# Four strided loads in place of one at the head of a streaming contrast kernel

## The chip, the cores and the metric

The kernel runs on one core of a Trainium2 chip. The metric is the device time of one execution in microseconds. Before the change the median of three runs is 239.16 us (239.13 to 239.31).

## The reference

The input is a batch of 16 images of 3 channels, 512 x 512 pixels in float32, 50.33 MB in all. For each of the 48 channel planes the mean is taken, and every pixel is moved away from it by a factor and clipped:

```python
def reference(x, factor):
    mean = np.mean(x, axis=(2, 3), keepdims=True)
    return np.clip(mean + factor * (x - mean), 0, 1).astype(np.float32)
```

Since factor * x + (1 - factor) * mean is the same thing, each pixel needs one multiplication and one addition of a number that is constant in its plane, and then a maximum and a minimum. The factor is 1.5.

## The kernel before

The input is seen as one long array of rows of 8192 elements (32 KB). A plane is 32 rows, and a tile is 128 rows, one to each partition of SBUF: four planes and 4 MB. There are 12 tiles. SBUF holds a ring of six of them (`ring`, 128 x 6 x 8192), so that tile t lies in slot t mod 6, and it is computed in place: the loaded slot is overwritten with the result and stored from there.

For each tile `compute(t)` does the following. VectorE adds up columns 0 to 4351 of each row (line 81), and ScalarE, beside it, columns 4352 to 8191 (line 84, whose elementwise output `junk` isn't used). Two small matrix products on TensorE (lines 86 and 87) with the block matrix `blockw`, which holds (1 - factor) / pixels in blocks of 32 x 32, add the row sums of each plane and give every row of the plane its number (1 - factor) * mean, in PSUM. VectorE then computes factor * x + that number (line 91) and the clip (line 94), and ScalarE's queue issues the store (line 101).

The first tile is cut in two. Its columns 0 to 2047 (`SHORT`, 8 KB of each row, 1 MB) are loaded by a DMA of their own, the other 6144 columns (3 MB) by a second, both from `load` (line 76) on SyncE's queue. Lines 91, 94 and 101 run over the same two parts for the first tile, so that the 1 MB part can be stored before the rest is done. The sums of line 81 reach over both parts.

The order of the work is written out by hand. SyncE issues, one behind the other and with nothing to wait for, the 1 MB and the 3 MB of tile 0, tile 1 (4 MB), tiles 2 and 3 in one DMA (8 MB), and tiles 4 and 5 in one DMA (8 MB). Then follows the loop over the tiles, in which each `compute(t)` is followed by the load of tile t + 6 into the slot that tile t leaves. That load waits on SyncE until the store of tile t has finished. All loads are on SyncE's queue, all stores on ScalarE's.

Each DMA signals its end on one of eight completion semaphores, which the framework hands out in turn over the loads and stores of both queues; a DMA that gets a semaphore for the second time waits until its earlier holder has ended.

Of the kernel before, what the change touches and what calls it, by code (L numbers as in the profile page):

```python
# [1 line left out]

# [4 lines left out]


P = 128  # L10
ROW = 8192
BUFS = 6
SHORT = 2048
FIRST = (SHORT, ROW - SHORT)
SUM = 4352


@with_exitstack
def kernel(
    ctx: ExitStack,  # L20
    tc: tile.TileContext,
    x: bass.AP,
    factor: float,
    out: bass.AP,
):

    nc = tc.nc
    f32 = mybir.dt.float32  # L30
    Alu = mybir.AluOpType
    Act = mybir.ActivationFunctionType

    B, C, H, W = x.shape
    n_img, n_pix = B * C, H * W
    ppi = n_pix // ROW
    per_tile = P // ppi
    n_tiles = n_img // per_tile
    assert ppi * ROW == n_pix and per_tile * n_tiles == n_img

    factor = float(factor)
    wconst = (1.0 - factor) / float(n_pix)

    x_f = x.rearrange("b c h w -> (b c h w)")
    out_f = out.rearrange("b c h w -> (b c h w)")

    def dram(ap, t, c0=0, c1=ROW):
        return bass.AP(tensor=ap.tensor, offset=t * P * ROW + c0, ap=[[ROW, P], [1, c1 - c0]])

    consts = ctx.enter_context(tc.tile_pool(name="consts", bufs=1))  # L50
    xpool = ctx.enter_context(tc.tile_pool(name="xpool", bufs=1))
    small = ctx.enter_context(tc.tile_pool(name="small", bufs=1))
    psum = ctx.enter_context(tc.tile_pool(name="psum", bufs=1, space=bass.MemoryType.PSUM))


    sums = small.tile([P, 2 * n_tiles], f32, name="sums")
    junk = small.tile([P, ROW - SUM], f32, name="junk")
    bias = psum.tile([P, n_tiles], f32, name="bias")

    blockw = consts.tile([P, P], f32, name="blockw")  # L60
    nc.gpsimd.memset(blockw, 0.0)  # L61
    for a in range(0, P, ppi):
        nc.gpsimd.memset(blockw[a : a + ppi, a : a + ppi], wconst)  # L63


    ring = xpool.tile([P, BUFS, ROW], f32, name="ring")

    def load(t, c0=0, c1=ROW, n=1):

        b = t % BUFS  # L70
        src = bass.AP(
            tensor=x_f.tensor,
            offset=t * P * ROW + c0,
            ap=[[ROW, P], [P * ROW, n], [1, c1 - c0]],
        )
        nc.sync.dma_start(out=ring[:, b : b + n, c0:c1], in_=src)  # L76

    def compute(t):
        xt = ring[:, t % BUFS, :]
        own = sums[:, 2 * t : 2 * t + 2]  # L80
        nc.vector.tensor_reduce(  # L81
            out=own[:, 0:1], in_=xt[:, 0:SUM], axis=mybir.AxisListType.X, op=Alu.add
        )
        nc.scalar.activation(out=junk, in_=xt[:, SUM:ROW], func=Act.Copy, accum_out=own[:, 1:2])  # L84
        shift = bias[:, t : t + 1]
        nc.tensor.matmul(shift, blockw, own[:, 1:2], start=True, stop=False)  # L86
        nc.tensor.matmul(shift, blockw, own[:, 0:1], start=False, stop=True)  # L87
        c = 0
        for n in FIRST if t == 0 else [ROW]:
            part = xt[:, c : c + n]  # L90
            nc.vector.tensor_scalar(  # L91
                out=part, in0=part, scalar1=factor, scalar2=shift, op0=Alu.mult, op1=Alu.add
            )
            nc.vector.tensor_scalar(  # L94
                out=part, in0=part, scalar1=0.0, scalar2=1.0, op0=Alu.max, op1=Alu.min
            )
            store(t, c, c + n)
            c += n

    def store(t, c0, c1):  # L100
        nc.scalar.dma_start(out=dram(out_f, t, c0, c1), in_=ring[:, t % BUFS, c0:c1])

    with tc.manual_schedule():
        load(0, c1=SHORT)
        load(0, c0=SHORT)
        load(1)
        load(2, n=2)
        load(4, n=2)
        for t in range(n_tiles):
            compute(t)  # L110
            if t + BUFS < n_tiles:
                load(t + BUFS)


# [1 line left out]
_INS = ['x', 'factor']  # L116
_OUTS = [((16, 3, 512, 512), 'float32')]

_NUMBERS = {'factor': 1.5}


# [26 lines left out]
```

## Time and profile before

The profile is one execution. It spans 237.3 us between its first and its last instruction; the 239.16 us are the median of three other executions, measured from outside.

| | before |
|---|---|
| median of three runs | 239.16 us |
| span of the profiled execution | 237.3 us |
| VectorE busy | 163.1 us (69%) |
| ScalarE busy | 43.2 us (18%) |
| TensorE busy | 14.1 us (6%) |
| bytes read and written | 50.33 MB and 50.33 MB |
| mean rate over the span | 424 GB/s |
| packets on the load queue, on the store queue | 1840, 1872 |
| share of 16 engines' span, loads and stores | 49.7%, 49.2% |

The page draws the span as 40 slices, and the digit of a slice is the share in tenths in which a unit was busy. A packet is what one DMA engine moves at a time: here a whole row of up to 32 KB, or a small write to a completion semaphore. The two queues' shares add up to 98.9% of the time that all 16 engines have.

Windows of the profile give, for stretches of the span, the busy time of each compute engine and then the DMA share and GB/s. A packet is counted there with its start, so that short windows swing above and below the true rate. The list of issues gives, for each group of DMAs, its size and the time from issue to landing. The chain of waits follows the work that ended last back from the last instruction; its lines have a start, a duration and what it was.

### The profile page before, as it was taken

The page shows a single profiled execution, that of the slowest core. Times are in us where ns is not written, and L with a number is a line of the kernel's source. Part 1 is how long each engine was busy: PE and PEld are TensorE (multiplying, and loading weights), DVE is VectorE, ACT ScalarE, POOL GpSimd, SP SyncE. Part 2 cuts the span into 40 slices and gives each one's busy share as a digit, 9 for nine tenths or more (in the row PEclk, how much of TensorE's full clock was granted, in tenths as well). Part 3 has the DMA queues.
Part 4 walks back from the last instruction along what each step waited for, and adds up shares of the span by engine and source line. Part 5 has one row for each costly group of instructions (what it writes and reads, how often), then busy time and mean ns, then how long its engine had stood idle before and what let it go on. Part 6 is the DMA issues. An engine that isn't in the chain of part 4 may idle for free.

```text
span 237.3 us, 285 instructions
## 1 busy us (share of the span) xinstructions
PE 14.1 (6%) x48; PEld 12.0 (5%) x48; DVE 163.1 (69%) x38; ACT 43.2 (18%) x25; POOL 0.9 (0%) x9
## 2 busy tenths in 40 slices
PE   0010010001010001010010100100100100010000
PEld 0010010001010001010010100100100100010000
DVE  0079989048989328999989898891892795687000
ACT  2050230041050023050320504101400500500000
POOL 1000000000000000000000000000000000000000
DMA  7999999999999999999999999999999999999996
GB/s 297 410 442 442 421 442 359 456 439 441 442 436 414 403 431 442 442 442 442 436 442 436 414 409 425 442 442 442 442 436 442 436 420 403 425 442 442 442 442 265
DMA packets 3712, 100.66 MB, mean 424 GB/s; under 512 B 384, under 2 KB 384, under 8 KB 384
## 3 DMA queue, kind: packets, MB, share of 16 engines
q1 hardware_dynamic: 1840, 50.33, 49.7%
q10 hardware_dynamic: 1872, 50.33, 49.2%
HBM read 50.33 MB, written 50.33 MB: 424 GB/s over the span
## 4 chain that ended last, share of the span: by engine, by line
DMA 57%; DVE 29%; another core or an unknown queue 3%; PE 1%; SPq 1%; issue 0%; DVEq 0%
DMA ring<-in_x_dram 41%; DMA out_dram<-ring 16%; DVE sums L81 10%; DVE ring L91 9%; DVE ring L94 9%; PE bias L87 1%; SPq L76 1%; DVEq L91 0%
## 5 line engine op out<-in xcount | busy, mean ns | idle before, releaser
L81 DVE TENSOR_REDUCE sums<-ring 128x1 f32<-128x4352 f32 x12 | 56.2, 4683 | 45.7 <-DMA ring<-in_x_dram 45.7
L84 ACT ACTIVATE junk<-ring 128x3840 f32<-128x3840 f32 x12 | 40.8, 3403 | 163.3 <-DMA ring<-in_x_dram 107.5
L91 DVE TENSOR_SCALAR ring<-ring,bias 128x8192 f32<-128x8192 f32 (+2 forms) x13 | 54.1, 4163 | 8.9 <-PE bias L87 7.4
L94 DVE TENSOR_SCALAR ring<-ring 128x8192 f32<-128x8192 f32 (+2 forms) x13 | 53.3, 4099 | 0.4
L86 PE MATMUL bias<-sums,blockw 128*128 128x1 f32 x24 | 7.0, 361 | 190.8 <-ACT junk L84 190.8
L86 PEld LDWEIGHTS bias<-sums,blockw 128*128 128x128 f32 x24 | 6.0, 312 | 191.7 <-ACT junk L84 175.2
L87 PE MATMUL bias<-sums,blockw 128*128 128x1 f32 x24 | 7.0, 363 | 4.3 <-DVE sums L81 3.9
L87 PEld LDWEIGHTS bias<-sums,blockw 128*128 128x128 f32 x24 | 6.0, 311 | 5.3 <-DVE sums L81 5.0
L84 ACT ACTIVATION_READ_ACCUMULATOR junk<-ring 128x1 f32 x12 | 2.2, 186 | 0.0
L84 ACT ACT_TABLE_LOAD x1 | 1.3, 1283 | 0.7 <-PEq L129 0.7
L63 POOL MEMSET blockw<- 32x32 f32 x4 | 0.5, 117 | 0.2
L61 POOL MEMSET blockw<- 128x128 f32 x1 | 0.2, 204 | 0.3 <-POOLq L129 0.3
L129 POOL MEMSET const-bfloat16-1.0<- 128x1 bf16 x1 | 0.1, 111 | 0.0
L129 POOL MEMSET const-uint8-127<- 128x1 uint8 x1 | 0.1, 111 | 0.0
L129 POOL MEMSET const-float32-1.0<- 128x1 f32 x1 | 0.1, 108 | 0.0
L129 POOL MEMSET const-float32-0.0<- 128x1 f32 x1 | 0.1, 103 | 0.2 <-issue 0.2
## 6 DMA issues: line engine op xcount, KB each, us to landing
out_dram<-ring ACTq DMA_DIRECT2D x11, 4096.0 KB, 35.8
ring<-in_x_dram SPq DMA_DIRECT2D x7, 4096.0 KB, 49.7
ring<-in_x_dram SPq DMA_DIRECT2D x2, 8192.0 KB, 66.7
ring<-in_x_dram SPq DMA_DIRECT2D x1, 3072.0 KB, 11.7
out_dram<-ring ACTq DMA_DIRECT2D x1, 3072.0 KB, 28.2
ring<-in_x_dram SPq DMA_DIRECT2D x1, 1024.0 KB, 4.8
out_dram<-ring ACTq DMA_DIRECT2D x1, 1024.0 KB, 17.5
```

The source lines that it names most:

```text
L61: nc.gpsimd.memset(blockw, 0.0)
L63: nc.gpsimd.memset(blockw[a : a + ppi, a : a + ppi], wconst)
L76: nc.sync.dma_start(out=ring[:, b : b + n, c0:c1], in_=src)
L81: nc.vector.tensor_reduce(out=own[:, 0:1], in_=xt[:, 0:SUM], axis=mybir.AxisListType.X, op=Alu.add)
L84: nc.scalar.activation(out=junk, in_=xt[:, SUM:ROW], func=Act.Copy, accum_out=own[:, 1:2])
L86: nc.tensor.matmul(shift, blockw, own[:, 1:2], start=True, stop=False)
L87: nc.tensor.matmul(shift, blockw, own[:, 0:1], start=False, stop=True)
L91: nc.vector.tensor_scalar(out=part, in0=part, scalar1=factor, scalar2=shift, op0=Alu.mult, op1=Alu.add)
L94: nc.vector.tensor_scalar(out=part, in0=part, scalar1=0.0, scalar2=1.0, op0=Alu.max, op1=Alu.min)
L129: nc = _bacc.Bacc("TRN2", target_bir_lowering=False, num_devices=1)
```

## The change

The 1 MB load of the first tile's columns 0 to 2047 is made by four DMAs of 256 KB. DMA number k takes rows k, k + 4, k + 8 and so on up to 128: 32 rows of 8 KB, which go to every fourth partition. The four are issued on the same queue, in the place of the one. All other loads, the stores and the computation are written as before, and the same bytes are moved to the same places.

```diff
@@ -13,6 +13,7 @@
 SHORT = 2048
 FIRST = (SHORT, ROW - SHORT)
 SUM = 4352
+STEP = 4
 
 
 @with_exitstack
@@ -75,6 +76,14 @@
         )
         nc.sync.dma_start(out=ring[:, b : b + n, c0:c1], in_=src)
 
+    def load_rows(k):
+        src = bass.AP(
+            tensor=x_f.tensor,
+            offset=k * ROW,
+            ap=[[STEP * ROW, P // STEP], [1, SHORT]],
+        )
+        nc.sync.dma_start(out=ring[k::STEP, 0, 0:SHORT], in_=src)
+
     def compute(t):
         xt = ring[:, t % BUFS, :]
         own = sums[:, 2 * t : 2 * t + 2]
@@ -101,7 +110,8 @@
         nc.scalar.dma_start(out=dram(out_f, t, c0, c1), in_=ring[:, t % BUFS, c0:c1])
 
     with tc.manual_schedule():
-        load(0, c1=SHORT)
+        for k in range(STEP):
+            load_rows(k)
         load(0, c0=SHORT)
         load(1)
         load(2, n=2)
```

## The prediction

> **What bounds the kernel now.** I read the share of the DMA engines over the span first, then the start and the end of the span in short windows, then the issues and the chain of waits.
>
> ```profile
> span 237.3 us, 285 instructions
> ...
> DMA  7999999999999999999999999999999999999996
> GB/s 297 410 442 442 421 442 359 456 439 441 442 436 414 403 431 442 442 442 442 436 442 436 414 409 425 442 442 442 442 436 442 436 420 403 425 442 442 442 442 265
> ```
>
> Between the first and the last fortieth the 16 DMA engines are never under nine tenths busy. The busiest compute engine, VectorE, has 69%. The packet records of the trace say it more sharply: from the first data packet at 1.74 us to the first engine that runs dry at 235.47 us, the idle time averages 0.24 us per engine, and all of it lies before 2.6 us. In steady state a 32 KB packet follows the one before it every 1.209 us on each engine, whether it loads or stores. So this kernel ends when 16 engines have moved 100.66 MB, and a wait on VectorE, ScalarE or SyncE counts only where it lets an engine run dry.
>
> ```profile
> 1.50:2.00 0.50, 0.00 (x0) 0.00 (x0) 0.00 (x0) 0.50 (x1) 0.08 (x1) 1.00 0.78 131
> 2.00:2.50 0.50, 0.00 (x0) 0.00 (x0) 0.00 (x0) 0.02 (x1) 0.00 (x0) 1.00 0.67 164
> 2.50:3.00 0.50, 0.00 (x0) 0.00 (x0) 0.00 (x0) 0.00 (x0) 0.00 (x0) 1.00 0.89 344
> 3.00:4.00 1.00, 0.00 (x0) 0.00 (x0) 0.00 (x0) 0.00 (x0) 0.00 (x0) 1.00 1.01 418
> ...
> 230.00:235.00 5.00, 0.00 (x0) 0.00 (x0) 0.00 (x0) 0.00 (x0) 0.00 (x0) 1.00 0.99 426
> 235.00:236.50 1.50, 0.00 (x0) 0.00 (x0) 0.00 (x0) 0.00 (x0) 0.00 (x0) 1.00 0.01 0
> ```
>
> The last two columns are DMA share and GB/s. The ramp from 1.5 to 3 us is the only place where engines give less than full rate for want of work, and the DMA that the change splits lies in it.
>
> ```profile
> ring<-in_x_dram SPq DMA_DIRECT2D x1, 3072.0 KB, 11.7
> ...
> ring<-in_x_dram SPq DMA_DIRECT2D x1, 1024.0 KB, 4.8
> ...
> L76 SPq DMA_DIRECT2D ring<-in_x_dram x11: 328/341/573, 0.7 to 154.2; - x11
> ...
> 0.74 0.37 SPq L76
> 1.12 0.05 issue
> 1.17 0.42 SPq L76
> 1.59 0.05 issue
> 1.64 0.42 SPq L76
> 2.06 0.04 issue
> 2.11 48.55 DMA ring<-in_x_dram
> ```
>
> SyncE issues its first loads one every 0.47 us. The 1 MB one, issued at 0.74, has landed 4.8 us later, at 5.5; the 3 MB one, issued at 1.17, at 12.9. VectorE and ScalarE start tile 0 on that second landing, not on the first.
>
> **The sum of before.** By the packet records each engine makes its eight 8 KB packets of the 1 MB load and then its completion write. The quickest engine writes it at 4.62 us, the median one at 4.86, the slowest at 5.19. At the end of the kernel the 16 engines finish between 235.47 and 236.04: the same spread of 0.57 us, 230.85 us later. The order of the engines at the start is carried rigidly to the end. So the span is 1.74 (before the first packet) + 3.45 (slowest engine's 1 MB) + 230.85 + 1.23 (last completion, closing barrier) = 237.27 us. The median of the runs, 239.16, is 1.89 us above it; I carry those 1.89 over unchanged.
>
> **The change part by part.** Only the first two terms can move, unless an engine runs dry later.
>
> *Bytes and packets.* The same 128 rows of 8 KB. Four completions replace one: three more small packets per engine. From the completion write to the next data packet the records show 6 ns (11.909 to 11.915): 3 x 6 = 0.02 us.
>
> *The first issue.* 32 rows in place of 128. It took 0.37 us and the first packet came 1.00 us after its start. The row of issues runs from 0.328 to 0.573 us, and its shortest ones are 128-row loads too, so I see no dependence on rows: 0, bounds -0.04 to +0.20.
>
> *SyncE's queue.* Three more DMAs at a 0.47 us pitch: the 3 MB load is issued at 2.62 instead of 1.17, load(1) at 3.1, load(2, n=2) at 3.6. Each small DMA gives an engine two packets, 2 x 0.309 = 0.62 us of work, and the next arrives 0.47 us later, so the engines stay fed. At the longest issue in the row (0.573 + 0.05) the margin is gone but nothing is lost. The 3 MB load must be there when the slowest engine needs it at 5.19 (the quickest at 4.62); issued at 2.62, with the 1.0 us of the first, it is there at 3.6. Cost 0. Without that cover, each late 0.1 us would be 0.1 us of span.
>
> *A new wait.* The eight completion semaphores go round the DMAs in program order, and with three more DMAs load(4, n=2) gets the one of the second small DMA: SyncE waits for that to land, about 5.5 us, where it issued at 2.72 before. Ahead of it in the queue are 16 MB, of which the last land at 50.65 (the chain above). Behind it on SyncE is load(6), issued at 55.96. So 45 us cover the wait. Every later DMA takes the semaphore of the DMA eight places before it, as it did; where that partner has changed it is one of the small loads, long landed.
>
> *The readers.* The first reduce on VectorE waits for five semaphores instead of two, and ScalarE before its first store for four instead of one: one more waiting instruction each, 0.03 us by the longest row of SyncE's (28 ns). They fall at 13 and 21 us, while the DMA engines work off queued loads. Cost 0.
>
> *The start of the stream.* This is the unknown, for no row of before has a load that takes every fourth partition. The first packets took 0.31 to 1.25 us where later ones take 0.309; the slowest engine lost 0.94 us there. Lower bound: that loss vanishes, and with it its late start, so that its completion comes at 1.70 + 8 x 0.306 = 4.15 instead of 5.19, -1.04 us. Upper bound: each of the three added DMAs makes a fresh start and loses the mean excess of a first packet (0.663 - 0.309 = 0.354 us), +1.06 us. The nearest row is the seam between the 1 MB and the 3 MB load, where the next data packet starts 6 ns after the completion write and takes its usual 0.912 us: no fresh start. I take 0.
>
> [...]
>
> **Sum.** completions +0.02, first issue 0, queue 0, new wait 0, readers 0, start of the stream 0: span 237.27 + 0.02 = 237.29, time 237.29 + 1.89 = 239.18, say 239.2 us. Its own range is within 0.2%, 238.7 to 239.6.
>
> **Rivals.**
>
> *Two engines at one place (slower).* If rows are dealt to the engines so that a 32-row load with a stride of four sends two engines to the same part of SBUF at once, the stream runs at half rate until the 1 MB is done: 8 packets x 0.309 = +2.47 us, 241.6; with the engines out of step by their first packets (0.7 us between their ends, two packets' worth) perhaps half, 240.4. It decides from the point where the four loads together need 0.48 us more than now, so that the slowest completion comes after 5.7 us. For it: the before kernel shows only 128-row transfers, so nothing proves the even deal. Against it: every fourth row over all 128 partitions spreads as widely as before.
>
> [...]
>
> *A fresh start for each small DMA (slower).* The upper bound above: +0.5 to +1.06, 239.7 to 240.2. The seam speaks against it; for it, that two packets per engine are little to run ahead with.
>
> *A quicker start (faster).* If smaller batches reach the 16 engines sooner and the slow first packets shrink, the slowest engine gains at least half of its 1.04 us: 238.1 to 238.7. For it: first packets start over 0.78 us (1.74 to 2.52). Against it: the slowest engines (3.02) had started at 1.77 and 2.05, so a late start isn't what made them slow, and the same cold rows are read first.
>
> *The split does nothing.* That is my forecast: the stream neither knows nor cares where one DMA ends.
>
> **How the numbers follow.** Runs of this kernel spread by 0.18 us; 0.2% is 0.48 us, about what a measurement can tell from no change. No change 0.45; shared place 0.28; fresh starts 0.10; quicker start 0.17. So faster 0.17, same 0.45, slower 0.38, and the time is that of the likeliest, 239.2. The range runs from half of the quicker start (238.6) to just under the full price of the shared place (241.5); some 12 in 100 lie outside.
>
> **What would show it.** Right: first packets at about 1.7 us, the completions of the four loads between 3 and 5.3 us, the 3 MB load landed at 12.9 +- 0.4, and the end of the packets 230.85 us after the slowest start. The shared place would show 8 KB packets near 0.6 us and a rate near 210 GB/s between 2.5 and 5 us; fresh starts, gaps or long packets at each seam; the quicker start, a landing of the 3 MB load before 12.4. I am wrong altogether if the front is unchanged and the time moves all the same, for then the order of loads and stores matters where I hold it rigid: some 40 load packets of over 1.3 us at 24 to 26 and 37 to 40 us are the one place with such slack, 0.8 us per engine in all.

## The result

The change makes the kernel slower. Six runs have a median of 242.75 us (241.01 to 243.47) against 239.23 us (239.11 to 239.49) for the kernel before, a ratio of 1.014 with a 95% interval of 1.0115 to 1.0164. Beside the loss of 3.5 us there is a second difference: the six runs of the changed kernel spread over 2.5 us, where the six of the kernel before beside them keep within 0.4.

First the page of the changed kernel, its span and the row of 40 slices:

```profile
span 241.1 us, 290 instructions
...
DMA  5999999999999999999999999999999999999992
GB/s 204 378 446 430 409 423 428 431 440 446 435 430 430 435 424 430 435 435 430 424 435 435 435 435 435 424 435 435 435 435 435 430 435 435 435 435 435 435 430 120
```

The middle is as full as before. Only the first slices and the last have changed: 204 and 378 GB/s at the head where there were 297 and 410, and 120 at the end in place of 265. The chain of waits of the changed kernel (start, duration, what it was) shows how the loads go out:

```profile
0.74 0.54 SPq L85
...
1.34 0.57 SPq L85
...
1.96 0.59 SPq L85
...
2.59 0.59 SPq L85
...
3.23 0.58 SPq L77
```

A load of every fourth row takes SyncE 0.54 to 0.59 us to issue, against 0.37 to 0.42 for the first loads before. One goes out every 0.62 us, and the 3 MB load leaves at 3.23 instead of 1.17. By the packet records the first data packet moves at 2.07 us instead of 1.74. The issues of the changed kernel, with their time to landing:

```profile
ring<-in_x_dram SPq DMA_DIRECT2D x1, 3072.0 KB, 12.9
...
ring<-in_x_dram SPq DMA_DIRECT2D x4, 256.0 KB, 3.5
```

So the 3 MB have landed at 3.23 + 12.9 = 16.1 us where it was 12.9: 3.2 of the 3.5 us are lost by then. Short windows of the changed kernel (the last two columns are DMA share and GB/s) show the two ends of the loss:

```profile
3.00:4.00 1.00, 0.00 (x0) 0.00 (x0) 0.00 (x0) 0.00 (x0) 0.00 (x0) 1.00 0.77 295
4.00:5.00 1.00, 0.00 (x0) 0.00 (x0) 0.00 (x0) 0.00 (x0) 0.00 (x0) 1.00 0.87 262
5.00:6.00 1.00, 0.00 (x0) 0.00 (x0) 0.00 (x0) 0.00 (x0) 0.00 (x0) 1.00 0.94 385
...
235.00:236.50 1.50, 0.00 (x0) 0.00 (x0) 0.00 (x0) 0.00 (x0) 0.00 (x0) 1.00 0.91 393
236.50:238.00 1.50, 0.00 (x0) 0.00 (x0) 0.00 (x0) 0.00 (x0) 0.00 (x0) 1.00 0.21 87
238.00:240.00 2.00, 0.00 (x0) 0.00 (x0) 0.00 (x0) 0.00 (x0) 0.00 (x0) 1.00 0.08 33
```

The same stretch of the kernel before:

```profile
4.00:5.00 1.00, 0.00 (x0) 0.00 (x0) 0.00 (x0) 0.00 (x0) 0.00 (x0) 1.00 1.49 631
5.00:6.00 1.00, 0.00 (x0) 0.00 (x0) 0.00 (x0) 0.00 (x0) 0.00 (x0) 1.00 0.97 418
...
236.50:238.00 1.50, 0.00 (x0) 0.00 (x0) 0.00 (x0) 0.00 (x0) 0.00 (x0) 1.00 0.00 0
```

From 3 to 5 us, where the kernel before was at full rate (418 GB/s in the first of these two), less than 300 GB/s flow (295 and 262). (The 631 is the start of many 24 KB packets that reach into the next window.) At the end the engines no longer finish together: from 236.5 us on a few work alone, and after 238 us about one or two in 16. The packet records give the same per engine. The 16 engines finish between 236.23 and 239.62 us, a spread of 3.39 us where it was 0.58. (An engine's completion of a load is the start of the small packet that it writes when its part is done.) Their completions of the 3 MB load have a mean of 14.08 us (12.14 before, +1.94) and a slowest of 15.74 (12.46 before, +3.28); the slowest completion of tile 1 is again 3.28 us later, and the very last of the kernel is 3.57 us later.

The 1.94 us of the mean engine come, by the same records, from four amounts: +0.27 us of idle time before 3 us (the later first packet), +0.78 us of idle time between 3 and 8.5 us, +0.90 us of packets longer than their usual time between 3 and 10 us, and -0.10 us at the first packets, which are a little quicker; they add up to 1.85. The rest of the slowest engine's 3.28, 1.3 us, is unevenness: some engines lose far more than the mean, and the kernel ends with the slowest.

### The profile page after: what moved, and what is told of

It reads as the page before. It is cut to its first block, busy times and chain, and to the rows that moved or that the text cites. A ratio compares the mean times of both kernels' runs of the same rounds, so it can differ in the third digit from the quotient of the medians.

```text
span 241.1 us, 290 instructions
## 1 busy us (share of the span) xinstructions
PE 14.1 (6%) x48; PEld 12.0 (5%) x48; DVE 163.1 (68%) x38; ACT 43.2 (18%) x25; POOL 0.9 (0%) x9
## 4 chain that ended last, share of the span: by engine, by line
DMA 57%; DVE 28%; another core or an unknown queue 3%; SPq 1%; PE 1%; issue 1%; DVEq 0%
DMA ring<-in_x_dram 40%; DMA out_dram<-ring 17%; DVE sums L90 10%; DVE ring L100 9%; DVE ring L103 9%; PE bias L96 1%; SPq L85 1%; SPq L77 0%; DVEq L100 0%
## 6 DMA issues: line engine op xcount, KB each, us to landing
ring<-in_x_dram SPq DMA_DIRECT2D x1, 3072.0 KB, 12.9
```

## The experiments

The theories are named as in the expectations. S: the engines run dry at the start, because a small load holds less work than the time until the next. P: the strided rows are slow in themselves or make two engines collide. N: each DMA costs its share wherever it stands. Each diff is against the changed kernel unless said otherwise. "Work" is what one engine has to do for a load, by the packet durations: 0.62 us for 256 KB in 8 KB packets, 0.64 in 2 KB packets, 1.24 for 512 KB.

**The strided loads behind the 3 MB (e1).**

```diff
+        load(0, c0=SHORT)
         for k in range(STEP):
             load_rows(k)
-        load(0, c0=SHORT)
```

> The same four strided 256 KB loads, issued behind the 3 MB load of tile 0 instead of ahead of it. Theory S (starved start: a small load gives an engine 0.6 us of work and takes 0.62 us to issue, engines run dry unevenly at the ramp and the slowest carries that to the end): the 3 MB keep every engine fed for 7 us, so the loss goes: 239.0 to 239.7 us, end spread of the 16 engines under 1 us. Theory P (the strided rows themselves are slow, or two engines collide in them): the loss stays, 241 to 243.5, with long packets where the strided loads run. Theory N (each DMA of this size costs a fixed amount wherever it stands): 241 to 243.

Measured: 239.61 us, ratio 1.0014 (1.0001 to 1.0027). No engine ran dry after the ramp, and the 16 ended within 0.57 us. The same four strided loads, with the same slow issue (0.52 to 0.61 us), cost next to nothing where each engine has 7 us of work ahead of them. P and N fall as explanations of the 3.5 us. The control, the kernel before with its two loads in that order (e8):

> The kernel before with its two loads of tile 0 in the other order, 3 MB first; no strided loads. It is the control of the experiment in which the strided loads stood behind the 3 MB (239.61). If the 0.4 us there came from the order: 239.5 to 239.7 here. If they came from the four strided loads: 239.1 to 239.3 here.

Measured: 239.41 us, ratio 1.0004 (0.9994 to 1.0014). It lies between the two expectations, and the intervals of e1 and e8 overlap: whether the remaining 0.2 us belong to the strided loads is not settled. The profiled execution of e8 was the longest of its ten (240.01 us); its engines ended with a spread of 1.37 us, although they had completed tile 0 within 0.52 us of each other.

**Two loads of every second row (e2).**

```diff
-STEP = 4
+STEP = 2
```

> Two loads of every second row (64 rows, 512 KB each) in place of four. Theory S: 1.24 us of work per engine and load against about 0.6 us to issue one, so engines stay fed; what is left is the later first packet, 0.3 us: 239.3 to 240.0. Theory P: the same strided share of 1 MB, 241 to 243. Theory N: one added DMA instead of three, a third of the loss: 240.2 to 240.6.

Measured: 240.15 us, 1.0043 (1.003 to 1.0057). Three quarters of the loss are gone with half the loads. It is a little over what S gave and just under N's figure, so it does not part those two alone; e1 does.

**Four loads of 32 neighbouring rows (e3).**

```diff
-            offset=k * ROW,
-            ap=[[STEP * ROW, P // STEP], [1, SHORT]],
+            offset=k * (P // STEP) * ROW,
+            ap=[[ROW, P // STEP], [1, SHORT]],
...
-        nc.sync.dma_start(out=ring[k::STEP, 0, 0:SHORT], in_=src)
+        nc.sync.dma_start(out=ring[k * (P // STEP) : (k + 1) * (P // STEP), 0, 0:SHORT], in_=src)
```

> Four loads of 32 neighbouring rows in place of every fourth row; number, size and place of the DMAs as in the changed kernel. Theory S with the stride to blame for the slow issue (0.54 to 0.59 us against 0.37 to 0.42): issues come at 0.47 us and the loss is at most half, 239.3 to 241. Theory S with the small load to blame: as the changed kernel, 241 to 243.5. Theory P in the form that the stride is bad: 239.3 to 240; in the form that engines collide on partitions: worse than the changed kernel, over 243.

Measured: 240.75 us, 1.0063 (1.0048 to 1.0078): slower than before and still 2 us faster than the changed kernel. Its chain of waits and its windows:

```profile
0.75 0.37 SPq L85
...
1.17 0.41 SPq L85
```

```profile
3.50:4.50 1.00, 0.00 (x0) 0.00 (x0) 0.00 (x0) 0.00 (x0) 0.00 (x0) 1.00 0.89 205
4.50:5.50 1.00, 0.00 (x0) 0.00 (x0) 0.00 (x0) 0.00 (x0) 0.00 (x0) 1.00 1.08 246
...
236.50:238.00 1.50, 0.00 (x0) 0.00 (x0) 0.00 (x0) 0.00 (x0) 0.00 (x0) 1.00 0.01 0
```

Two things are to be seen. The issue is quick again (0.37 and 0.41 us), so it is the stride, of the rows and the partitions together, and not the 32 rows, that lengthens it. And the DMA engines are busy throughout at about half the rate (205 and 246 GB/s): the 8 KB packets take 0.58 us in the median, where they take 0.31 with every fourth row. Packets near 0.6 us and a rate near 210 GB/s are what the first rival expected, and here they come in a kernel without its stride. Whether two engines meet at one place there is not shown. Slow as they are, these loads hold about 1.2 us of work each. No engine runs dry, and all end within 0.68 us of each other.

**Four loads of all rows, 512 columns each, on one queue (e4) and on two (e11).**

```diff
-            load_rows(k)
+            load(0, c0=k * SHORT // STEP, c1=(k + 1) * SHORT // STEP)
```

> Four loads of all 128 rows, 512 columns (2 KB) each: the same number of DMAs and bytes, no strided rows, four times as many packets, of a quarter the size. Theory S: an engine gets 8 x 2 KB, again about 0.6 us of work; if the issue takes 0.47 us as 128-row loads do, nearly fed: 239.3 to 240.5. Theory P: no strided rows, no loss: 239.0 to 239.6. Theory N: as the changed kernel, 241 to 243.5.

Measured: 241.54 us, 1.0101 (1.0077 to 1.0124). No stride is left, the loads go out every 0.47 us and hold 0.64 us of work, and 2.3 us are lost. So S is wrong as it was put: the comparison of issue time with work isn't the rule. e11 is e4 with loads 1 and 3 issued by ScalarE:

```diff
-    def load(t, c0=0, c1=ROW, n=1):
+    def load(t, c0=0, c1=ROW, n=1, queue=nc.sync):
...
-            load_rows(k)
+            load(0, k * SHORT // STEP, (k + 1) * SHORT // STEP, 1, nc.scalar if k % 2 else nc.sync)
```

> The four loads of 512 columns, issued in turn by SyncE and ScalarE. With one queue they cost 2.3 us although they were issued every 0.47 us and hold 0.64 us of work. If it is the queue (one load after another on the same queue can't flow sooner than about 1.2 us apart), two queues bring it to 239.2 to 240.2. If it is the short lists themselves or the 2 KB packets, it stays: 241 to 242.5.

Measured: 239.48 us, 1.0013 (1.0004 to 1.0022). The same loads in the same pieces lose 0.3 us instead of 2.3 when no queue has more than two of them. The second queue also lets the 3 MB go out sooner: SyncE issued it at 1.64 us instead of 2.58. Which of the two counts, e11 alone doesn't tell. Windows of e4 first, then of e11:

```profile
5.00:6.00 1.00, 0.00 (x0) 0.00 (x0) 0.00 (x0) 0.00 (x0) 0.00 (x0) 1.00 0.97 283
...
235.00:236.50 1.50, 0.00 (x0) 0.00 (x0) 0.00 (x0) 0.00 (x0) 0.00 (x0) 1.00 0.31 131
236.50:238.00 1.50, 0.00 (x0) 0.00 (x0) 0.00 (x0) 0.00 (x0) 0.00 (x0) 1.00 0.05 22
```

```profile
5.00:6.00 1.00, 0.00 (x0) 0.00 (x0) 0.00 (x0) 0.00 (x0) 0.00 (x0) 1.00 1.16 494
...
235.00:236.50 1.50, 0.00 (x0) 0.00 (x0) 0.00 (x0) 0.00 (x0) 0.00 (x0) 1.00 0.01 0
```

The dip at 5 to 6 us, mostly long packets, and the ragged end go together, and both are gone with two queues.

**The strided loads on two queues (e5).**

```diff
-    def load_rows(k):
+    def load_rows(k, queue):
...
-        nc.sync.dma_start(out=ring[k::STEP, 0, 0:SHORT], in_=src)
+        queue.dma_start(out=ring[k::STEP, 0, 0:SHORT], in_=src)
...
-            load_rows(k)
+            load_rows(k, nc.scalar if k % 2 else nc.sync)
```

> The changed kernel with its four strided loads issued in turn by SyncE and ScalarE, two each, so that a new one comes every 0.3 us instead of every 0.62; everything else as in the changed kernel. Theory S (engines run dry because a strided load takes as long to issue as an engine takes for its two packets): now twice as much work is offered as is done, the loss shrinks to the later first packet: 239.3 to 240.3, end spread under 1 us. Theory Q (it is the small load itself, two packets and a completion per engine with a read-ahead that starts anew, whoever issues it): 241 to 243.5.

Measured: 240.18 us, 1.004 (1.0025 to 1.0055), end spread 0.73 us. As with the columns, most of the loss goes; the first packet still starts at 2.07 us.

**More work in each strided load (e6, e7).** In e6 the four loads take columns 0 to 4095 and the second load of tile 0 the rest; in e7 they take whole rows and there is no second load. The diff is that of e7; e6 has columns 0 to 4095 in the places of the whole row, and keeps the second load from column 4096 on.

```diff
-            ap=[[STEP * ROW, P // STEP], [1, SHORT]],
+            ap=[[STEP * ROW, P // STEP], [1, ROW]],
...
-        nc.sync.dma_start(out=ring[k::STEP, 0, 0:SHORT], in_=src)
+        nc.sync.dma_start(out=ring[k::STEP, 0, :], in_=src)
...
-        load(0, c0=SHORT)
```

> Four strided loads of 16 KB of each row (512 KB each) instead of 8 KB; the second load of tile 0 takes the other 16 KB. Theory S: 1.2 us of work per engine and load against 0.62 us of issue: fed, only the later first packet of 0.34 us is left: 239.4 to 240.2. Theory Q: two packets and a completion as before, still four times: 241 to 243.

> Tile 0 loaded by four strided loads of whole rows (1 MB each), with no second load of tile 0. Theory S: 2.4 us of work per engine and load: fed, 239.3 to 239.9 (the later first packet, 0.34 us). Theory P (strided rows are slow in themselves): four times the bytes, over 245. Theory Q: four short lists of two packets: 241 to 243.

Measured: e6 240.51 us, 1.0052 (1.0037 to 1.0067), a little over S's figure; e7 239.72 us, 1.0018 (1.0009 to 1.0028), with all 16 engines ending within 0.26 us. With the number of strided loads the same, the loss falls from 3.5 over 1.2 to 0.4 us as an engine's work per load goes from 0.6 over 1.2 to 2.4 us. What is left in e7 is about the 0.33 us of the later first packet.

**The changed kernel again (e9).**

> The changed kernel once more, unaltered, for a second profile and for times on the same chip as the next three. If the uneven engines are chance at the ramp, the time again varies by 1 us and more between runs (241 to 243.5) and the end spread of the 16 engines is 1.5 us or more, with another amount than the 3.4 us of the first profile. If it is a fixed fault of one engine, spread and time repeat within 0.3 us.

Measured: 242.87 us (242.33 to 243.41), 1.0154 (1.0139 to 1.0168), end spread 2.71 us. The packet records again show an early hole, from 3.7 to 4.4 us, before the third load flows, and then one or two engines far behind: two start their fourth small load at 6.5 and 7.0 us. In the first profile one did, at 6.8, and one began the 3 MB only at 7.4. The form of the loss repeats, the amount varies.

**Two loads of 1024 columns (e10).** As e4, with STEP = 2.

> Two loads of all 128 rows, 1024 columns each (512 KB, 1.24 us of work per engine), no strided rows. Theory S in the form 'each load must carry an engine over the time until the next one flows, about 1.2 us': no dry engines, and without the later first packet of the strided form: 239.1 to 239.7, about 0.4 us under the two strided loads (240.15). If any split of the first load costs its share (theory N): 240.0 to 240.6.

Measured: 239.33 us, 1.0008 (0.9999 to 1.0017): no loss that can be told from none. N falls here too. The two strided loads of the same size (e2) cost 0.8 us more, more than their later first packet.

**The order of three loads (e13, e14) and one small load alone (e15).** All rows, one queue, columns cut at 512 and 1024 (e13), at 1024 and 1536 (e14), at 512 (e15):

```diff
-STEP = 4
+CUTS = (0, 512, 1024, 2048)
...
-        for k in range(STEP):
-            load_rows(k)
+        for c0, c1 in zip(CUTS, CUTS[1:]):
+            load(0, c0=c0, c1=c1)
```

> The first 2048 columns in three loads of all rows on one queue: 512, 512 and 1024 columns. Theory H (the third load on a queue can't flow before about 2.4 us after the first packet, so the two loads ahead of it must hold that much work): 1.28 us of work ahead of the third, engines stall about 0.6 to 1 us, some more: 239.8 to 240.9. Theory L (each small load costs its share, 0.77 us, wherever it stands): two of four small loads, 240.2 to 240.5, and the same as in the next experiment.

> The same three loads with the large one first: 1024, 512, 512 columns. Theory H: 1.88 us of work ahead of the third and 2.5 us ahead of the fourth, hardly a stall: 239.2 to 239.8. Theory L: 240.2 to 240.5, the same as with the small ones first.

> Two loads of all rows: 512 columns, then 1536. Theory H: only 0.64 us of work in the first, but the third load on the queue (3 MB) has 2.5 us ahead of it: no stall, 239.1 to 239.6. Theory L: one of four small loads, 239.8 to 240.1.

Measured: e13 241.64 us, 1.0093 (1.0078 to 1.0109); e14 239.9 us, 1.0023 (1.0013 to 1.0032); e15 239.59 us, 1.0008 (0.9999 to 1.0018). The ends in windows, of e13 and then of e14:

```profile
235.00:236.50 1.50, 0.00 (x0) 0.00 (x0) 0.00 (x0) 0.00 (x0) 0.00 (x0) 1.00 0.46 197
236.50:238.50 2.00, 0.00 (x0) 0.00 (x0) 0.00 (x0) 0.00 (x0) 0.00 (x0) 1.00 0.04 16
```

```profile
235.00:236.50 1.50, 0.00 (x0) 0.00 (x0) 0.00 (x0) 0.00 (x0) 0.00 (x0) 1.00 0.11 44
236.50:238.50 2.00, 0.00 (x0) 0.00 (x0) 0.00 (x0) 0.00 (x0) 0.00 (x0) 1.00 0.00 0
```

The same three loads cost 2.3 us with the two small ones first and 0.6 with the large one first. Theory L, a share for each small load, wants the same time for both and falls. Theory H has the direction, and one small load at the head is nearly free, as it says; but its figure for e13 (239.8 to 240.9) was too low.

The packet records narrow this down. By the completion of tile 0 the mean engine has lost the same in both, 0.88 us in e13 and 0.94 in e14. What differs is the slowest engine (1.59 and 0.95 us later than before) and what follows: the very last completion is 2.23 us later in e13 and 0.34 in e14. So the order didn't remove the loss at the head; it kept the engines together, and e14 got most of its loss back later. Between 20 and 50 us the kernel before has 41 packets of 32 KB that take over 1.3 us, in all 0.74 us per engine more than the usual 1.21 each; in e13 that is 0.32 us, in e14 0.05.

**One load for tile 0 (e12).** Against the kernel before: `load(0)` in place of its two loads.

> The kernel before with tile 0 loaded by one 4 MB load. In the experiment with whole strided rows the 16 engines ended within 0.26 us of each other, against 0.58 us in the kernel before, although its first packet was 0.34 us later. If the end is the slowest engine's start carried through, the first packet at 1.74 us and that small spread give a slowest end of about 235.7 instead of 236.04: 238.8 to 239.1 us, slightly faster than the kernel before. If the first packet's size or the extra 1 MB load don't matter: 239.1 to 239.4.

Measured: 239.78 us, 1.0027 (1.0015 to 1.0038): slower, not faster. Its slowest engine ended at 236.22 us, with a spread of 0.65, so the small spread of e7 doesn't come from the long first packets. Its profiled execution took 2.5 us more than its span, where the others took 1.9 to 2.2; why is not known. No version tried beats the kernel before.

Set side by side by the work that stands ahead of the third load of SyncE's queue (counting what ScalarE loads beside it), the loss against the kernel before is as follows. The middle column is from one profiled execution each: how much later than before tile 0 was complete, on the mean of the 16 engines and on the slowest.

| kernel | work ahead of the third load | tile 0 later: mean, slowest | loss |
|---|---|---|---|
| changed (e9) | 2 x 0.62 = 1.2 us | 2.4, 3.4 us | 3.7 us |
| e4, 512 columns | 2 x 0.64 = 1.3 us | 1.2, 1.9 us | 2.3 us |
| e13, small ones first | 1.3 us | 0.9, 1.6 us | 2.3 us |
| e14, large one first | 1.24 + 0.64 = 1.9 us | 0.9, 0.9 us | 0.6 us |
| e3, neighbouring rows | 4 x 0.58 = 2.3 us | 1.8, 1.7 us | 1.6 us |
| e6, strided 512 KB | 2.5 us | 1.2, 1.5 us | 1.2 us |
| e2, strided 512 KB, then 3 MB | 2.5 us | 0.5, 0.4 us | 1.0 us |
| e5, strided, two queues | 4 x 0.62 = 2.5 us | 0.4, 0.6 us | 0.9 us |
| e10, e11, e15, all rows | 2.5 us | 0.1 to 0.2, -0.1 to 0.2 us | 0.1 to 0.3 us |
| e7, strided 1 MB | 2 x 2.4 = 4.9 us | 0.5, 0.4 us | 0.4 us |

With loads of all rows the loss is down to 0.1 to 0.3 us at 2.5 us of work; the strided ones, whose first packet is 0.33 us later, still lose 0.9 to 1.2 us there and 0.4 at 4.9, and those of e3 have slow packets of their own (0.58 us). This order is a fit to the rows, not a mechanism that a run shows. e14 and e10 have the same 2.5 us of work ahead of the 3 MB load, and e14 loses 0.9 us at the head where e10 loses 0.1.

## Why the prediction was wrong

**What bounds the kernel** was right, and for the changed kernel so was the rigid carry, nearly: the slowest engine's completion of the 3 MB comes 3.28 us later, and so does that of tile 1; the end comes 3.57 us later. It isn't a rule: in e3 the slowest engine is 1.69 us late at tile 0 and 0.99 at the end, in e14 0.95 and 0.34, in e13 1.59 and 2.23. The long packets between 20 and 50 us, which the prediction named as the one place with slack, are nearly gone in e3 and e14.

**Bytes, the new wait, the readers** held. SyncE's wait for the second small load did not lengthen anything that shows: load(4, n=2) left at 4.80 us, far ahead of need.

**The first issue** took 0.54 instead of 0.37 us, and 1.33 us instead of 1.00 passed to the first packet: with +0.33 us the term lies outside its bounds of -0.04 to +0.20. I saw "no dependence on rows", and e3 bears that out (32 neighbouring rows, 0.37 us); the dependence is on the stride (0.54), which no row of before had. By e7 this term is worth 0.33 to 0.39 us.

**SyncE's queue is the step that failed.** It said that each small load gives an engine 0.62 us of work "and the next arrives 0.47 us later, so the engines stay fed", at no cost. The pitch was 0.62, with no margin left; the prediction allowed for that and held that nothing would be lost. More than that, the comparison itself was wrong: in e4 the pitch was 0.47 against 0.64 us of work, and 2.3 us were lost all the same. What the packet records show in place of the cost of 0: between 3 and 8.5 us the mean engine stood idle for 0.78 us, its packets took 0.90 us longer than usual, and the slowest engine came out of tile 0 3.28 us late. With a second queue (e11), larger loads (e10, e7) or 3 MB ahead (e1) 0.1 to 0.4 us of the loss are left, and with a large load first (e14) 0.6. The times fit a condition, that the third load of a queue wants about 2.5 us of work ahead of it; why it would is not shown.

**The start of the stream** was bounded by +1.06 us, three fresh starts at the mean excess of a first packet, and taken as 0 by the seam between the 1 MB and the 3 MB load. That seam was not the nearest row it seemed: its second load had been queued for 3.5 us, behind 2.5 us of work, when it was needed. And the bound took the mean of 16 engines where the slowest counts: the mean engine lost 1.94 us, the slowest 3.28. Had the bound gone by the longest first packet of before (0.94 us over its usual time), three of them would have given 2.8 us.

**The rivals.** The fresh start for each small load came nearest in kind, with a chance of 0.10 and a price of at most a third of the true one. Two engines at one place, the one I held likelier, was not what happened: the median 8 KB packet of the changed kernel takes 0.309 us, as before. Packets of nearly twice that came with neighbouring rows (0.58 us, e3). The half rate of two engines at one place was my estimate, and that such a meeting makes those packets is not shown. The quicker start is there in the first packets, and it is worth 0.10 us.

What stays open is what holds the third load back. In both profiles of the changed kernel nearly every engine also has one long packet of the 3 MB load between 6.5 and 8.5 us, 1.0 to 2.3 us instead of 0.91, many of them with no idle time before. That is not a late issue, and no run here shows what it is. The records of the other runs add where it occurs: 16 to 28 of the 128 packets of the 3 MB load take over 1.0 us where that load is the fourth or fifth of its queue and comes behind at most 1 MB (the changed kernel twice, e3, e4, e13, e14), and none to two where it is the third (e2, e5, e10, e11, e15) or, in the kernel before, the second. (As the very first load, in e1 and e8, it has 18 and 17, at the start of the stream.) So the number of loads ahead may count as much as the work in them; the two were not varied apart at the head.

## What to carry to other kernels

In this kernel, which keeps its DMA engines full to the end, what the head of the stream lost reached the end, and the slowest engine counted rather than the mean: it completed tile 0 3.28 us late, the mean engine 1.94, and the last completion came 3.57 us later. Look at the spread of the last completions and compare it with that of the first loads: in the changed kernel it was made in the first microseconds, in the profiled execution of e8 it was not. Here it paid to start a queue with larger loads (two of 1.24 us of work each lost 0.1 us, four of 0.64 us 2.3), and to put small ones behind a large one (0.6 us in e14, 2.3 in e13) or on a second queue (0.3 us in e11, 2.3 in e4). An issue pitch shorter than the work of a load does not prove that the engines stay fed (e4: 0.47 against 0.64 us); look for a row in which a load was needed as soon after its issue as the new one will be.

## What the runs showed of the hardware

Loads of every second or fourth row, into as many partitions, took SyncE 0.52 to 0.69 us to issue at the head of the kernel, those of neighbouring rows of one tile 0.36 to 0.43, for 32 as for 128 rows. The first ordinary load behind strided ones was as long as they were (0.58 us for the 3 MB load of the changed kernel), the one after it was not (0.43).

A second queue was worth 2.1 us without any byte less (e4 and e11). The issue time saved was 0.94 us (the 3 MB left at 1.64 instead of 2.58 us), and the gain was more than twice that; what the rest of it comes from is not shown.

The cost of small loads changed with their order: 256, 256 and 512 KB cost 2.3 us (e13), 512, 256 and 256 KB cost 0.6 (e14). The mean engine lost 0.9 us at the head in both.
